# Second FFN product and output projection of three token blocks on 512 columns at a time, in four PSUM banks of their own, in one kernel of a hybrid RWKV-7/S5 layer

## The chip, the cores and the metric

The kernel runs on one core of a Trainium2 chip. The metric is device time in microseconds (us) of one execution. The engines are TensorE (PE in the rows, with PEld for its weight loads), VectorE (DVE), ScalarE (ACT), GpSimd (POOL) and SyncE (SP), whose queue issues the DMAs. PSUM, in which matmuls accumulate, has eight banks, each of 128 partitions x 512 fp32 values.

## The reference, cut to what matters

One layer with the same weights on 256 context tokens and 2048 latent tokens, model width 1024. The mixer has two head groups: a bidirectional RWKV-7 recurrence (8 heads of 64) and a bidirectional S5 with a gated linear unit. Then:

```
# mixer: rwkv_x = (groupnorm(y_fwd + y_bwd) + bonus) * (sigmoid(gd) @ g2); s5_x = z * sigmoid(z @ glu_w + glu_b)
x = x + mod_x[2] * (concatenate([rwkv_x, s5_x], -1) @ w_out)          # w_out 1024 x 1024
h = modulate(rmsnorm(x, norm2_g), mod_x[3], mod_x[4])
x = x + mod_x[5] * ((silu(h @ w1) * (h @ w3)) @ w2)                   # w1, w3 1024 x 2816, w2 2816 x 1024
return rmsnorm(x, final_g)
```

The outputs are the 2048 latent rows in fp32. To keep precision each large product is made of three reduced-precision ones: both factors are split into a high and a low part, and high x high, high x low and low x high are added up in the same bank.

## The kernel before

The change lies in the last part of the program, the class `Tail`. The 2048 latent tokens are taken as four blocks of 512, from block 3 down to block 0. For each block there are these steps:

- **readout(b)**, in eight pieces: reads the scan's result from DRAM (tiles yl, pl, vl), normalises it by heads, adds the bonus and multiplies with the gate. A piece takes three banks: pcv (L1213 on high and low parts for the mean, later transposes), pb and pg.
- **outproj(b)** and **norm(b)**: the product with w_out is added to X1 (the residual, token rows on the partitions), squares are summed on the way, and `rms` makes the reciprocal root. GpSimd puts it on a diagonal (tile nt, L1340), TensorE multiplies it with X1, which also transposes (L1347), VectorE applies scale and shift (L1349) and the result is split into tiles H and L, the ffn's input.
- **ffn(b)**: 22 pieces f of 128 hidden columns. A piece has 2 x 24 matmuls of 512 columns for w1 and w3 (L1371, tiles p), then silu, multiplication and a split into gh and gl. Pieces come in parts, `SPLITS` = f 0-3, 4-7, 8-11, 12-15, 16-19 and 20-21, and each part ends with its share of the second product.
- **final(b)**: the last norm and the store.

Both products, w_out and w2, go through `product`. It walks over the 1024 output columns in four steps of 256 (cq). In a step two banks hold four 128 x 256 results, and each contraction step k loads and splits a 128 x 256 piece of weights (vr, vh, vl2) and issues 4 x 3 matmuls of 256 columns (L1295 to L1297). At the end of a step VectorE multiplies with the gate (L1300) and GpSimd adds into X1 (L1303).

The banks: pool `fp` has four, under one name "f", handed out in the order in which the program asks. The w1/w3 tiles and `product` take theirs there. When the scan's banks have been given up (`rwkv.close()`), `aside` brings four more, pool `fq`; from then on readout and norm of blocks 2 to 0 take theirs from `fq`.

The order of the work: the last twelve units of the RWKV scan (R.unit, L1005 to L1082 among its lines) are written first, then parts 0 to 2 of ffn(3). Then comes, for b = 3, 2, 1: parts 0 to 2 of ffn(b) (unless b is 3), the readout of block b - 1 with parts 3 and 4 of ffn(b) written between its pieces, outproj(b - 1), norm(b - 1), part 5 of ffn(b) and final(b). ffn(0) stands at the end. A scheduler lays out each engine's instruction row from this text before the kernel runs: an instruction may be put ahead of others if its tiles and banks can be had by then, and banks of one pool go to the users in the order of the text. On the chip an engine's row is fixed.

Of the kernel before, what the change touches and what calls it, by code (L numbers as in the profile page):

```python
# [9 lines left out]
F32 = mybir.dt.float32  # L10
F32R = mybir.dt.float32r
I32 = mybir.dt.int32
AF = mybir.ActivationFunctionType
OP = mybir.AluOpType
# [1094 lines left out]
class Tail:  # L1109


    def __init__(self, tc, I, K, S, out, f1, fp):
        self.tc, self.nc, self.I, self.K, self.S, self.out = tc, tc.nc, I, K, S, out
        self.f1, self.fp = f1, fp
        self.side = (f1, fp, "t", "s", "gh", "gl")
        self.C, self.H, self.X = {}, {}, {}
        nc, blk, ident = self.nc, K["blk"], K["ident"]
        self.Cm = f1.tile([P, P], F32, name="Cm")
        nc.vector.scalar_tensor_tensor(self.Cm, blk, -1.0 / 64, ident, op0=OP.mult, op1=OP.add)
        self.RK = f1.tile([P, 4, P], F32, name="RK")  # L1120
        for hp in range(4):
            nc.vector.tensor_scalar(self.RK[:, hp], blk, V(K, "rwkv_rk", hp), None, op0=OP.mult)
        self.gb = f1.tile([P, 4], F32, name="gb")
        o = VOFF["s5_glu_b"]
        nc.vector.tensor_scalar(self.gb, K["vec"][:, o:o + 4], 0.5, None, op0=OP.mult)
        self.g2 = f1.tile([96, 512], F32, name="g2")
        nc.sync.dma_start(self.g2, I["rwkv_g2"][0])

    def aside(self, f2, fq):

        self.side = (f2, fq, "nt", "ns", "zh", "zl")
        nc = self.nc
        self.ER = f2.tile([P, 2, P], F32R, name="ER")
        nc.scalar.activation(self.ER[:, 0], self.Cm, AF.Copy)
        nc.scalar.activation(self.ER[:, 1], self.K["blk"], AF.Copy)
        self.GR = f2.tile([96, 2, 512], F32R, name="GR")
        self.split(self.GR[:, 0], self.GR[:, 1], self.g2)
# [61 lines left out]
    def readout(self, b, put):  # L1199
# [26 lines left out]
        for hf in range(2):  # L1226
# [7 lines left out]
            for hp in range(4):  # L1234
# [35 lines left out]
                put(b, hp, ts, s)  # L1270
                yield

    def product(self, b, A, n, wsrc, grow, last):


        nc, f1 = self.nc, self.f1
        mm = nc.tensor.matmul
        X1 = self.X[b]
        for cq in range(4):
            cols = slice(256 * cq, 256 * cq + 256)  # L1280
            gq = f1.tile([P, 256], F32, name="gq", bufs=2)
            nc.sync.dma_start(gq, bcast_row(grow[cols], 256))
            po = [self.ftile([P, 2, 256]) for _ in range(2)]
            for k in range(n):
                with self.tc.high_priority(offset=1000):
                    raw = f1.tile([P, 256], F32, name="vr", bufs=3)
                    nc.sync.dma_start(raw, wsrc(k, cols))
                    vh = f1.tile([P, 256], F32R, name="vh", bufs=2)
                    vl = f1.tile([P, 256], F32R, name="vl2", bufs=2)
                    self.split(vh, vl, raw)  # L1290
                ah, al = A[k]
                for j in range(4):
                    o = po[j // 2][:, j % 2]
                    js = slice(j * P, (j + 1) * P)
                    mm(o, ah[:, js], vh, start=k == 0 and j % 2 == 0, stop=False)  # L1295
                    mm(o, ah[:, js], vl, start=False, stop=False)  # L1296
                    mm(o, al[:, js], vh, start=False, stop=k == n - 1 and j % 2 == 1)  # L1297
            for u in range(2):
                t = f1.tile([P, 2, 256], F32, name="t", bufs=2)
                nc.vector.tensor_tensor(t, po[u], gq[:, None, :].to_broadcast([P, 2, 256]), op=OP.mult)  # L1300
                for j in range(2):
                    x = X1[2 * u + j][:, cols]
                    nc.gpsimd.tensor_tensor(x, x, t[:, j], op=OP.add)  # L1303
                    if last:
                        self.square(b, 2 * u + j, cq, t[:, j])

    def square(self, b, j, cq, junk):
        if (b, "ss") not in self.X:
            self.X[b, "ss"] = self.f1.tile([P, 4, 4], F32, name="sq", bufs=2)
        x = self.X[b][j][:, 256 * cq:256 * cq + 256]  # L1310
        self.nc.scalar.activation(junk, x, AF.Square, accum_out=self.X[b, "ss"][:, j, cq:cq + 1])  # L1311

    def rms(self, b):
# [19 lines left out]
    def norm(self, b):  # L1333
# [8 lines left out]
        HL = pool.tile([P, 8, 512], F32R, name="L")  # L1342
        self.H[b] = HH, HL
        for kc in range(8):
            pt = self.ftile(None, fq)
            for j in range(4):
                nc.tensor.matmul(pt[:, j * P:(j + 1) * P], self.X[b][j][:, kc * P:(kc + 1) * P], dg[:, j], start=True, stop=True)  # L1347
            tmp = f2.tile([P, 512], F32, name=tag_s, bufs=2)
            nc.vector.tensor_scalar(tmp, pt, mod[:, 4, kc:kc + 1], mod[:, 5, kc:kc + 1], op0=OP.mult, op1=OP.add)  # L1349
            self.split(HH[:, kc], HL[:, kc], tmp)  # L1350
# [59 lines left out]
def hybrid_block(tc, I, out):  # L1410
    with tc.tile_pool(name="dram", bufs=1, space=bass.MemoryType.DRAM) as dp, \
# [50 lines left out]
        with tc.tile_pool(name="f1", bufs=1, side="right") as f1, tc.tile_pool(name="fp", bufs=4, space=PSUM, side="right") as fp:  # L1462
# [13 lines left out]
                R.unit(h, h < 0 or False, pe_add=False)  # L1476
            run(T.ffn(3, SPLITS[:3]))
            rwkv.close()
            with tc.tile_pool(name="f2", bufs=1) as f2, tc.tile_pool(name="fq", bufs=4, space=PSUM) as fq:
                T.aside(f2, fq)  # L1480
                for b in (3, 2, 1):
                    if b < 3:
                        run(T.ffn(b, SPLITS[:3]))
# [33 lines left out]
```

## Time and profile before

| | us |
|---|---|
| median of three runs | 3780.82 |
| lowest, highest | 3780.75, 3784.65 |
| the profiled execution, its own time | 3786.86 |
| span of the profiled execution | 3785.1 |
| TensorE busy in the span | 3332.9 (88%) |
| VectorE busy | 2496.0 (66%) |
| GpSimd busy | 1831.6 (48%) |
| ScalarE busy | 1722.3 (46%) |

The mean granted TensorE clock of the profiled execution is 0.907 of full speed. Times in the rows are counted from the start of the span. A matmul's busy time runs from its start to its modelled end; the next ones may have started by then. In a timeline a row stands for consecutive alike instructions, with the start of the first, the time from there to the end of the last and, after x, their number. The scan ends at about 2317 us; behind it the blocks 2 to 0 fill the rest.

### The profile page before, as it was taken

To read this page: it belongs to the slowest core of one execution; us is meant where nothing else is said; L and a number is where in the kernel's file an instruction comes from. 1 tells how busy PE (TensorE), PEld (TensorE's weight loads), DVE (VectorE), ACT (ScalarE), POOL (GpSimd) and SP (SyncE) were. 2 spreads that over 40 slices of the span, in tenths; PEclk is the share of its full clock that TensorE was granted. 3 is DMA by queue.
4 is the path that set the end of the run, shared out by engine and by line. 5 is a ranking of instruction groups with operands and counts; after the bars stand their busy time and mean duration, and the time that the engine had idled before them with its cause. 6 is when DMAs were issued, how large, how long until landed. Compare 5 with 4: busy or idle time off the path is not lost. (4 is left out here: it accounts for less than half of the span.)

```text
span 3785.1 us, 70325 instructions
## 1 busy us (share of the span) xinstructions
PE 3332.9 (88%) x25311; PEld 2769.1 (73%) x25311; DVE 2496.0 (66%) x4726; ACT 1722.3 (46%) x3787; POOL 1831.6 (48%) x3184
## 2 busy tenths in 40 slices
PE   5798888888677776688899999999999999999998
PEld 3676666666556555566677888888889888988887
DVE  7668777776879978757766656576444854454444
ACT  3575656555344323554555644353333533343333
POOL 3366658576777656467667663323112321221212
PEclk9798989999767787678899999999999999999999
DMA  6654545554334443166533335454333533334333
GB/s 187 186 135 116 147 116 142 134 145 123 91 105 130 134 136 99 48 165 148 136 97 94 104 97 151 121 169 127 99 98 102 176 104 103 105 100 120 103 99 95
DMA packets 789020, 462.34 MB, mean 122 GB/s; under 512 B 182544, under 2 KB 766868, under 8 KB 788672
## 3 DMA queue, kind: packets, MB, share of 16 engines
q1 hardware_dynamic: 788672, 457.85, 43.3%
q8 instruction: 200, 3.28, 0.4%
q14 instruction: 148, 1.21, 0.1%
HBM read 382.34 MB, written 75.36 MB: 121 GB/s over the span
## 5 line engine op out<-in xcount | busy, mean ns | idle before, releaser
L1303 POOL TENSOR_TENSOR X<-X,t 128x256 f32<-128x256 f32 x464 | 379.0, 845 | 970.4 <-DVE t L1300 963.8
L999 POOL TENSOR_TENSOR tmp<-AT,T 128x60 f32<-128x60 f32 (+24 forms) x992 | 398.9, 402 | 186.2 <-DVE AT L992 85.6
L1144 DVE TENSOR_TENSOR wl<-wr,wh 128x512 fp32r<-128x512 f32 x368 | 270.7, 737 | 278.8 <-PE f L1371 238.2
L1001 POOL TENSOR_TENSOR T<-T,tmp 128x60 f32<-128x60 f32 (+24 forms) x992 | 416.7, 420 | 67.4
L1144 DVE TENSOR_TENSOR vl<-vr,vh 128x256 fp32r<-128x256 f32 x480 | 262.3, 550 | 273.9 <-ACT vh L1143 273.4
L1143 ACT ACTIVATE wh<-wr 128x512 fp32r<-128x512 f32 x368 | 232.2, 632 | 408.5 <-PE f L1371 370.3
L1296 PE MATMUL f<-vl,gh 128*128 128x256 f32 x1408 | 396.1, 289 | 13.6 <-DVE vl L1144 13.5
L1371 PE MATMUL f<-H,wh 128*128 128x512 f32 x1408 | 390.1, 396 | 8.3 <-ACT wh L1143 8.0
L1143 ACT ACTIVATE vh<-vr 128x256 fp32r<-128x256 f32 x480 | 199.3, 417 | 430.5 <-PE f L1297 382.3
L1371 PE MATMUL f<-H,wl 128*128 128x512 f32 x1408 | 389.8, 396 | 5.0 <-DVE wl L1144 4.9
L1371 PE MATMUL f<-L,wh 128*128 128x512 f32 x1408 | 390.5, 394 | 0.0
L1297 PE MATMUL f<-vh,gl 128*128 128x256 f32 x1408 | 388.8, 285 | 0.0
L1295 PE MATMUL f<-vh,gh 128*128 128x256 f32 x1408 | 361.6, 287 | 4.3 <-ACT vh L1143 4.2
L255 DVE SCALAR_TENSOR_TENSOR acc<-zb,cw,acc 128x512 f32<-128x512 f32 (+2 forms) x384 | 317.2, 842 | 26.2 <-ACT acc L251 21.3
L1371 PEld LDWEIGHTS f<-H,wl 128*128 128x128 f32 x1408 | 260.1, 188 | 62.8 <-DVE wl L1144 7.1
L1371 PEld LDWEIGHTS f<-L,wh 128*128 128x128 f32 x1408 | 261.7, 188 | 57.3
L1371 PEld LDWEIGHTS f<-H,wh 128*128 128x128 f32 x1408 | 256.9, 188 | 62.3 <-ACT wh L1143 9.5
L1296 PEld LDWEIGHTS f<-vl,gh 128*128 128x128 f32 x1408 | 269.7, 192 | 25.0 <-DVE vl L1144 18.4
L1297 PEld LDWEIGHTS f<-vh,gl 128*128 128x128 f32 x1408 | 269.9, 192 | 2.7
L1295 PEld LDWEIGHTS f<-vh,gh 128*128 128x128 f32 x1408 | 252.7, 191 | 13.1 <-ACT vh L1143 6.3
L222 PE MATMUL pa<-HI,wl 128*128 128x512 f32 (+1 forms) x712 | 208.2, 413 | 59.3 <-POOL wl L219 39.1
L222 PE MATMUL pa<-HI,wh 128*128 128x512 f32 (+1 forms) x712 | 217.6, 428 | 18.4 <-ACT wh L218 12.3
(459 smaller groups left out, 7391.1 us busy)
## 6 DMA issues: line engine op xcount, KB each, us to landing
wr<-in_ffn_w_dram SPq DMA_DIRECT2D x352, 256.0 KB
raw<-in_w_in_dram SPq DMA_DIRECT2D x178, 256.0 KB
vr<-in_ffn_w_dram SPq DMA_DIRECT2D x352, 128.0 KB
ld<-s_rkvk SPq DMA_DIRECT2D x36, 768.0 KB
mraw<-in_mod_w_dram SPq DMA_DIRECT2D x64, 256.0 KB
vr<-in_w_out_dram SPq DMA_DIRECT2D x128, 128.0 KB
gq<-s_gate SPq DMA_DIRECT2D x116, 128.0 KB
SV<-s_vt SPq DMA_DIRECT2D x144, 64.0 KB
```

Of the source, the lines that this page charges most:

```text
L222: nc.tensor.matmul(pa[:, :nt], w[:, kc, :], h[:, 4 * kh + kc, :nt], start=kh + i + kc == 0, stop=kh == 1 and i == 2 and kc == 3)
L255: nc.vector.scalar_tensor_tensor(ag, zb[:, i0 - 1 + a:i0 - 1 + a + nr, e:e + 64], tap(a, e), ag, op0=OP.mult, op1=OP.add)
L999: eng.tensor_tensor(tv, AT[:, l + 1:, l:l + 1].to_broadcast([P, n, m]), T[:, l:l + 1, 0:m].to_broadcast([P, n, m]), op=OP.mult)
L1001: eng.tensor_tensor(T[:, l + 1:, 0:m], T[:, l + 1:, 0:m], tv, op=OP.add)
L1143: self.nc.scalar.activation(hi, x, AF.Copy)
L1144: self.nc.vector.tensor_tensor(lo, x, hi.bitcast(F32), op=OP.subtract)
L1295: mm(o, ah[:, js], vh, start=k == 0 and j % 2 == 0, stop=False)
L1296: mm(o, ah[:, js], vl, start=False, stop=False)
L1297: mm(o, al[:, js], vh, start=False, stop=k == n - 1 and j % 2 == 1)
L1303: nc.gpsimd.tensor_tensor(x, x, t[:, j], op=OP.add)
L1371: mm(p, a[:, kc, :], h[:, 4 * kh + kc, :], start=kh + i + kc == 0, stop=kh == 1 and i == 2 and kc == 3)
```

## The change

`product` gets a second form, `wide`, which all calls for blocks 2 to 0 use once `aside` has run; block 3 keeps the narrow one. `wide` walks over the output columns in two steps of 512. Its four 128 x 512 results each have a bank of their own, o0 to o3, in a pool `fo` that replaces `fq`; each has one buffer. Weights come in 128 x 512 pieces (wr, wh, wl in f2), and a contraction step issues 4 x 3 matmuls of 512 columns. `norm` takes its banks from o0 to o3, too. `readout` of blocks 2 to 0 now takes its banks from `fp`, together with w1 and w3. The sums of squares have two columns for a row of X1 where there were four.

```diff
-    def aside(self, f2, fq):
-
-        self.side = (f2, fq, "nt", "ns", "zh", "zl")
+    def aside(self, f2, fo):
+
+        self.side = (f2, self.fp, "nt", "ns", "zh", "zl")
+        self.fo = fo
...
+    def wide(self, b, A, n, wsrc, grow, last):
+
+        nc, f1, f2 = self.nc, self.f1, self.side[0]
+        mm = nc.tensor.matmul
+        X1 = self.X[b]
+        for cq in range(2):
+            cols = slice(512 * cq, 512 * cq + 512)
+            gq = f2.tile([P, 512], F32, name="gw", bufs=2)
+            nc.sync.dma_start(gq, bcast_row(grow[cols], 512))
+            po = [self.fo.tile([P, 512], F32, name="o%d" % j) for j in range(4)]
+            for k in range(n):
+                with self.tc.high_priority(offset=1000):
+                    raw = f2.tile([P, 512], F32, name="wr", bufs=3)
+                    nc.sync.dma_start(raw, wsrc(k, cols))
+                    vh = f2.tile([P, 512], F32R, name="wh", bufs=2)
+                    vl = f2.tile([P, 512], F32R, name="wl", bufs=2)
+                    self.split(vh, vl, raw)
+                ah, al = A[k]
+                for j in range(4):
+                    js = slice(j * P, (j + 1) * P)
+                    mm(po[j], ah[:, js], vh, start=k == 0, stop=False)
+                    mm(po[j], ah[:, js], vl, start=False, stop=False)
+                    mm(po[j], al[:, js], vh, start=False, stop=k == n - 1)
+            for j in range(4):
+                t = f1.tile([P, 512], F32, name="t", bufs=2)
+                nc.vector.tensor_tensor(t, po[j], gq, op=OP.mult)
+                x = X1[j][:, cols]
+                nc.gpsimd.tensor_tensor(x, x, t, op=OP.add)
+                if last:
+                    self.square(b, j, cq, t, 512)
+
     def product(self, b, A, n, wsrc, grow, last):
 
 
+        if self.fo and b < 3:
+            return self.wide(b, A, n, wsrc, grow, last)
         nc, f1 = self.nc, self.f1
...
-            pt = self.ftile(None, fq)
+            pt = self.fo.tile([P, 512], F32, name="o%d" % (kc % 4)) if self.fo else self.ftile()
...
-            with tc.tile_pool(name="f2", bufs=1) as f2, tc.tile_pool(name="fq", bufs=4, space=PSUM) as fq:
-                T.aside(f2, fq)
+            with tc.tile_pool(name="f2", bufs=1) as f2, tc.tile_pool(name="fo", bufs=1, space=PSUM) as fo:
+                T.aside(f2, fo)
```

The lines of the changed kernel have other numbers: L1213 becomes L1215 (readout), L1371 becomes L1406 (w1 and w3), L1347 becomes L1382 (norm), and L1295 to L1297 are now the wide matmuls.

The change moves instructions on TensorE's row in two places of interest. The first is the end of the scan. Before, w1/w3 matmuls of ffn(3) (L1371, tiles f, H and L with wh and wl) stand between those of the last scan unit (L1014, L1021, L1052):

```order
L1371 MATMUL f<-L,wh 128x512 x4
L1014 MATMUL p<-tmp,AY 32x32 x16
L1371 MATMUL f<-H,wl 128x512 x4
L1371 MATMUL f<-H,wh 128x512 x4
L1371 MATMUL f<-L,wh 128x512 x4
L1371 MATMUL f<-H,wl 128x512 x4
L1371 MATMUL f<-H,wh 128x512 x4
L1371 MATMUL f<-L,wh 128x512 x3
L1021 MATMUL p<-TW_1082,T_22200 32x32 x16
L1371 MATMUL f<-L,wh 128x512
```

After, the same unit's matmuls follow one another directly, and the first of readout(2) (L1215) stand behind them, ahead of the next of ffn(3) (L1406):

```order
L1021 MATMUL p<-TW_1085,T_22529 32x32 x16
L1052 MATMUL p<-R,TW_1085 64x64 x8
L1061 MATMUL c<-UV,BT 64x64 x8
L1074 MATMUL p<-AR,UV 64x64 x8
L1076 MATMUL p<-Q,SV 64x64 x8
L1047 MATMUL c<-SV,Q 64x64 x8
L1052 MATMUL p<-R,TW_1085 64x64 x8
L1074 MATMUL p<-AR,UV 64x64 x8
L1076 MATMUL p<-Q,SV 64x64 x8
L1215 MATMUL f<-rh,ER 128x256 x2
L1215 MATMUL f<-sh,GR 128x256
L1406 MATMUL f<-H,wh 128x512 x4
```

What moved are the w1/w3 matmuls of ffn(3) and the narrow product that belongs to them, from between the scan's matmuls to behind the first readout matmuls.

The second place is the end of outproj(1), TensorE again. Before, w1/w3 and narrow product matmuls of ffn(2) (L1371, and L1295 to L1297 with gh and gl) stand between the last matmul of outproj(1) and the first of norm(1) (L1347):

```order
L1297 MATMUL f_31830<-vh_31959,L_29565 128x256
L1371 MATMUL f_32162<-H_27108,wh_32183 128x512 x2
L1371 MATMUL f_32162<-L_27109,wh_32183 128x512 x4
L1371 MATMUL f_32162<-H_27108,wl_32184 128x512 x4
L1371 MATMUL f_32199<-H_27108,wh_32202 128x512 x4
L1371 MATMUL f_32199<-L_27109,wh_32202 128x512 x4
L1371 MATMUL f_32199<-H_27108,wl_32203 128x512 x4
L1295 MATMUL f_32245<-vh_32249,gh_32158 128x256
```

After, the norm's first matmul (L1382, in bank o0) follows directly on the last wide one of outproj(1) (bank o3):

```order
L1297 MATMUL o2_30429<-wh_30559,L_28789 128x512
L1296 MATMUL o3_30430<-wl_30560,H_28788 128x512
L1297 MATMUL o3_30430<-wh_30559,L_28789 128x512
L1382 MATMUL o0_30613<-nt_30606,X1_30250 128x128
L1382 MATMUL o1_30622<-nt_30606,X1_30250 128x128
```

What moved are the remaining matmuls of ffn(2)'s last part: those of w1 and w3 stand further up, those of its second product behind the norm's.

## Rows read from the trace of the kernel before

**Rows 1.** Stretches, core 0: length, then busy us (count) by engine, clock, DMA.
```profile
core 0: us, PE busy (x) PEld busy (x) DVE busy (x) ACT busy (x) POOL busy (x), PEclk, DMA share, GB/s
2226.00:2324.00 98.00, 97.55 (x885) 82.53 (x885) 47.75 (x88) 42.40 (x94) 50.68 (x124) 1.00 0.33 97
2324.00:2420.00 96.00, 89.33 (x553) 78.37 (x552) 72.46 (x198) 43.52 (x100) 36.64 (x45) 1.00 0.57 168
2420.00:3750.00 1330.00, 1315.47 (x7887) 1164.63 (x7887) 706.84 (x1351) 493.30 (x1080) 313.56 (x390) 1.00 0.39 114
1895.00:1900.00 5.00, 4.47 (x67) 3.99 (x64) 3.19 (x11) 1.66 (x4) 3.02 (x10) 0.55 0.08 22
```

**Rows 2.** Page, costliest groups: busy us, mean ns | idle before, releaser.
```profile
L1296 PE MATMUL f<-vl,gh 128*128 128x256 f32 x1408 | 396.1, 289 | 13.6 <-DVE vl L1144 13.5
...
L1371 PE MATMUL f<-H,wh 128*128 128x512 f32 x1408 | 390.1, 396 | 8.3 <-ACT wh L1143 8.0
```

**Rows 3.** TensorE's timeline, ffn(0): start, us, instruction, count.
```profile
3498.03 1.09 PE L1371 MATMUL f<-L,wh 128*128 128x512 f32 x4
...
3501.76 0.28 PE L1295 MATMUL f<-vh,gh 128*128 128x256 f32 x1
...
3506.21 0.28 PE L1295 MATMUL f<-vh,gh 128*128 128x256 f32 x1
...
3508.13 0.28 PE L1296 MATMUL f<-vl,gh 128*128 128x256 f32 x1
```

**Rows 4.** TensorE's timeline, end of the scan and first readout matmul.
```profile
2253.60 1.18 PE L1014 MATMUL p<-tmp,AY 32*32 32x32 f32 x32
...
2291.79 1.18 PE L1014 MATMUL p<-tmp,AY 32*32 32x32 f32 x32
...
2315.76 0.68 PE L1076 MATMUL p<-Q,SV 64*64 64x64 f32 x16
...
2323.98 0.28 PE L1213 MATMUL f<-rh,ER 128*128 128x256 f32 x1
```

**Rows 5.** Timelines of ScalarE and GpSimd there; in brackets idle time before.
```profile
2250.70 0.69 ACT L1005 ACTIVATE tmp<-T 128x256 f32<-128x256 f32 x1
...
2255.02 0.47 POOL L999 TENSOR_TENSOR tmp<-AT,T 128x31 f32<-128x31 f32 x1 [6.09 <-PE p L1014]
...
2282.05 0.66 ACT L1005 ACTIVATE tmp<-T 128x256 f32<-128x256 f32 x1 [4.46 <-DVE T L1004]
...
2316.48 0.77 ACT L1082 ACTIVATE YW<-p 64x256 f32<-64x256 f32 x2 [0.82 <-PE p L1076]
```

**Rows 6.** TensorE's timeline, a scan unit without filler and norm(3).
```profile
1886.25 0.28 PE L1297 MATMUL f<-vh,L 128*128 128x256 f32 x1
...
1898.64 1.04 PE L1076 MATMUL p<-Q,SV 64*64 64x64 f32 x16
...
1899.62 0.38 PE L1347 MATMUL f<-t,X 128*128 128x128 f32 x1
```

**Rows 7.** TensorE's timeline, end of outproj(1) and start of norm(1).
```profile
2921.64 0.28 PE L1297 MATMUL f<-vh,L 128*128 128x256 f32 x1
...
2921.76 0.63 PE L1371 MATMUL f<-H,wh 128*128 128x512 f32 x2
...
2931.13 0.50 PE L1347 MATMUL f<-nt,X 128*128 128x128 f32 x3
```

**Rows 8.** Timelines of VectorE and GpSimd in the same place.
```profile
2921.36 1.29 DVE L1300 TENSOR_TENSOR t<-f,gq 128x512 f32<-128x512 f32 x2 [0.31 <-PE f L1297]
...
2922.14 3.51 POOL L1303 TENSOR_TENSOR X<-X,t 128x256 f32<-128x256 f32 x4 [22.77 <-DVE t L1300]
...
2933.57 1.53 DVE L1349 TENSOR_SCALAR ns<-f,modv 128x512 f32<-128x512 f32 x2 [0.57 <-PE f L1347]
...
2948.27 0.68 DVE L1144 TENSOR_TENSOR L<-ns,H 128x512 fp32r<-128x512 f32 x1
```

**Rows 9.** TensorE's timeline, its last matmul.
```profile
3768.82 0.28 PE L1297 MATMUL f<-vh,gl 128*128 128x256 f32 x1
```

More of the change, by code (lines that the diff above doesn't have):

```diff
@@ L1115, in __init__ @@
         self.side = (f1, fp, "t", "s", "gh", "gl")
+        self.fo = None
         self.C, self.H, self.X = {}, {}, {}
@@ L1305, in product, with square @@
                         self.square(b, 2 * u + j, cq, t[:, j])
-    def square(self, b, j, cq, junk):
+    def square(self, b, j, cq, junk, n=256):
         if (b, "ss") not in self.X:
-            self.X[b, "ss"] = self.f1.tile([P, 4, 4], F32, name="sq", bufs=2)
-        x = self.X[b][j][:, 256 * cq:256 * cq + 256]
+            self.X[b, "ss"] = self.f1.tile([P, 4, 4], F32, name="sq", bufs=2)[:, :, 0:D // n]
+        x = self.X[b][j][:, n * cq:n * cq + n]
         self.nc.scalar.activation(junk, x, AF.Square, accum_out=self.X[b, "ss"][:, j, cq:cq + 1])
```

## The prediction

> **What bounds the kernel now.** I first read the stretches table [rows 1]. From 2420 us to 3750 us TensorE is busy for 1315.47 of 1330 us at full granted clock, so in the stage that the change rewrites the time is TensorE's pace, and only 14.5 us of idle time are there to win. In 2226 to 2324 us, the end of the scan, it is just as full (97.55 of 98). Behind that, in 2324 to 2420 us, it is idle for 6.7 us. So two questions decide: does the wide product need fewer TensorE us, and does TensorE still find work in the places where it now has none to spare?
>
> The groups table [rows 2] answers the first wrongly if read as it stands: 289 ns for a 256-column matmul and 396 for a 512-column one make 2 x 289 - 396 = 182 ns for each pair replaced, some 390 us over 2160 pairs. These durations overlap, since matmuls are pipelined. The timeline gives the pace from start to start [rows 3]: 16 matmuls of 512 columns take 3501.76 - 3498.03 = 3.73 us, 0.2333 each; 16 of 256 columns take 3508.13 - 3506.21 = 1.92 us, 0.120 each.
>
> **The pace.** Each of blocks 2, 1, 0 has 22 + 8 = 30 contraction steps of 4 x 4 x 3 = 48 narrow matmuls: 4320 in all, which become 2160 wide. A pair costs 0.240 us, a wide one 0.2333: 0.0067 x 2160 = 14.4 us. The small gaps that the narrow stream shows at bank changes add 1 or 2: I take -16, bounds -10 and -22.
>
> Here a page can be set beside the row. The Trainium skill, "TensorE: Matmul & The Clock Gate", section "Back-to-back issue gap", gives 262 cycles for 256 columns and 518 for 512; at 2.4 GHz two minus one is 6 cycles, 2.5 ns, an estimate of 5.4 us for 2160 pairs. The trace shows 6.7 ns where the page has 2.5; the measurement decides, and both are far below the 182 ns of the groups table.
>
> **The end of the scan.** In the trace of before TensorE fills the waits of the last two scan units with the fourth part of ffn(3), f12 to f15 (48 matmuls of 512 each), its narrow product (192 of 256) and 14 matmuls of f16: (192 + 14) x 0.2333 = 48.1, plus 192 x 0.120 = 23.0, together 71.1 us, all ahead of the first readout matmul of block 2 at 2323.98 [rows 4]. After the change the readout takes its banks from the pool of four that ffn uses, and that part of ffn(3) was written behind the first readout step. The first place of the order shows the result: in the new order no ffn matmul stands among the last units' matmuls; L1406 comes only behind L1215. TensorE takes its row in order, so these 71 us are done later, and the scan's end runs bare.
>
> How much earlier does it end, bare? From the rows of the engines beside it [rows 4, 5]: the input of the last but one unit's L1014 is ready at 2250.70 + 0.69 = 2251.4. L1014 and its follower start 1.4 us apart (2253.60 to 2255.02). GpSimd's inverse runs from 2255.02 until ScalarE hands on its result at 2282.05: 27.0, and the copy 0.7. Then L1014 and L1021 of the last unit, in the trace 8.1 us with 28 large matmuls (6.5) between them, bare 2 x 1.18 + 2 x 0.66 = 3.7. Then L1052 to the last L1076: the same chain ran nearly bare before norm(3), from 1886.25 to 1898.64 + 1.04 [rows 6], 13.4. The copy 2316.48 + 0.77, and from there to the first readout matmul, through DRAM, 2323.98 - 2317.25 = 6.7. Sum: 2251.4 + 1.4 + 27.0 + 0.7 + 3.7 + 13.4 + 0.8 + 6.7 = 2305. So the readout starts 19 us earlier and 71.1 us of TensorE work lie behind it: +52. Bounds: +41, if the bare chain ends at 2294 because GpSimd and VectorE, with fewer splits to share, run it a tenth faster; +71, if it ends no earlier.
>
> **The norms.** Between the last outproj matmul of block 1 (2921.64) and the first of its norm (2931.13) lie 9.5 us, in which VectorE scales, GpSimd adds the residual [rows 8], ScalarE squares and the reciprocal root is formed. In the trace TensorE works right through it, on w1/w3 matmuls of ffn(2), in other banks [rows 7]. While VectorE then turns norm banks into the next block's input (2933.57 to 2948.27 [rows 8]), it works on the narrow product of ffn(2).
>
> After the change w1/w3 of f20 and f21 stand ahead of the second half of outproj, and the wide product of ffn(b, last part) needs banks o0 to o3, which the norm takes first. The second place of the order shows the last L1297 with L1382 right behind it; norm(0) has the same. TensorE's only choice is to wait. The price of one: the chain, 9.5, plus 1.5 because four multiplications and four 512-column additions are still to come after the last matmul where two and four narrower ones were, = 11; then some 4 us in the norm phase (eight bank reads at about 0.77 each, with splits between, against 3.74 us of L1347), less the 1.5 that stand there now: 13.5. Twice that is +27. Norm(2) keeps 80 narrow matmuls of block 3 as cover, 9.6 us: +4. The nearest bare row, norm(3), has 13.4 us from its last outproj matmul to its first L1347 [rows 6], so the bounds for all three are +20 and +40.
>
> **Smaller terms.** Readouts now compete with the w1/w3 tiles for four banks, and a readout bank is held through a chain of ScalarE and VectorE steps: +6, bounds 0 and +20 (24 steps of under 1 us). Of the deferred work some can fill the 6.7 us that are idle behind readout(2) [rows 1]: -6, bounds 0 and -10. Where TensorE had been mostly idle the granted clock was 0.55 in the next 5 us (1895 to 1900 [rows 1]), and full in the stage behind: three new idle stretches give +3, bounds 0 and +10. At the end, 16.3 us lie between the last matmul (3768.82 [rows 9]) and the end of the span; four last additions of 512 columns instead of 256 are left over: +1, bounds -1 and +3.
>
> **Costed at nothing.** Weight loads of 256 KB in place of 128, half as many issues on SP: that queue is not late in the stage, and a wide step lasts 24 x 0.2333 = 5.6 us. The splits of a 512 step (about 0.7 us on either engine) run under the same 5.6 us. The o banks are single: at the change of column step four multiplications of 0.69 us stand against the next step's first matmuls, whose bank is the first one freed, 12 matmuls (1.4 to 2.8 us) after it was finished. If that cover failed, it would cost about 1 us at each of some 20 changes; this is in the upper bound.
>
> **The sum**, against the profiled execution's own 3786.86 us: -16 + 52 + 27 + 4 + 6 - 6 + 3 + 1 = +71, 3858. The profiled execution stands 6 us above the median of the runs shown (3780.82), so the forecast is **3852 us**, 1.9% slower.
>
> **Rivals.** (1) *TensorE loses no work time*, the faster side: the deferred 71 us and the norms' waits fit into time that was idle anyway, or TensorE passes by a waiting matmul; only the pace is left, 3781 - 16 = 3765. It decides if idle time behind 2324 us exceeds about 80 us; the rows show 6.7 + 14.5 = 21 [rows 1], and in the bare stretch before norm(3) nothing of another sort ran on TensorE between the chain's matmuls and L1347 [rows 6]. The Trainium skill, "TensorE: Matmul & The Clock Gate", section "Step-by-step: what each phase is for", has matmuls in program order, with only weight loads drawn ahead; the trace agrees there, with 13.4 us between the last outproj matmul and L1347 [rows 6]. Chance 6 in 100.
> (2) *It nets out*: the pace is worth 22, the scan ends 30 us earlier, and the norms are half covered; about 3781, against three rows at once. 3 in 100.
> (3) *Norms covered*: squares, sums and the ident scaling finish under the last matmuls, so that the 31 us fall away; 3820. For it: the multiplications now come in larger pieces. Against it: nothing stands between the two lines in the order. 10 in 100.
> (4) *Worse*: the scan ends no earlier (+71 where I have +52), norms 40, clock 10, readouts 10: 3852 + 19 + 9 + 7 + 4 = 3891, up to some 3900. 14 in 100.
> The forecast itself, 3820 to 3880, has 67.
>
> **How the numbers follow.** About 0.2%, 7.5 us, is what a measurement of this kernel tells from no change. Faster: rival 1, 0.06; same: rival 2, 0.03; slower: the rest, 0.91. For the range, leaving out rivals 1 and 2 and half of rival 4 leaves some 16 in 100 out: 3806 to 3892, of which the lower end stands for the covered norms with a cheaper scan end (3820 less 14).
>
> **What would show it.** In the new trace: the first L1215 of block 2 near 2305 us, with TensorE well under half busy in the 50 us before it; two idle stretches of 10 us or more directly before L1382, and one of about 4; 0.233 us from start to start in the wide stream; TensorE's idle time from there to the end at some 50 to 60 us where it was 21. A first L1215 near 2324 means rival 4, one before 2280 or ffn matmuls among the last scan rows means that the largest term is wrong. No idle time ahead of L1382 means rival 3. A time under 3780 would say that the order on TensorE isn't what sets the time here.

## The result and the profile after

| | before | after |
|---|---|---|
| median, us | 3782.39 (4 runs) | 3829.48 (3826.88 to 3835.88, 4 runs) |
| ratio, 95% interval | | 1.0129, 1.0114 to 1.0145 |
| span of the profiled execution, us | 3785.1 | 3834.0 |
| TensorE busy, us | 3332.9 (88%) | 3312.2 (86%) |

The changed kernel is 47 us slower. The forecast was 71 us slower, 3852, with a range from 3806 to 3892.

The stretches of the changed kernel (columns as in [rows 1]): the first three answer to those of before, the other three lie around the start of norm(1).

```profile
core 0: us, PE busy (x) PEld busy (x) DVE busy (x) ACT busy (x) POOL busy (x), PEclk, DMA share, GB/s
2226.00:2324.00 98.00, 56.74 (x601) 47.58 (x601) 38.98 (x90) 34.74 (x83) 42.52 (x124) 0.76 0.33 105
2324.00:2420.00 96.00, 94.21 (x526) 81.10 (x525) 57.16 (x142) 37.68 (x80) 25.16 (x30) 1.00 0.41 120
2420.00:3750.00 1330.00, 1298.50 (x5897) 1060.20 (x5896) 696.90 (x1201) 452.86 (x837) 286.79 (x244) 0.99 0.38 114
...
2970.00:2975.00 5.00, 0.03 (x1) 0.00 (x0) 2.96 (x3) 2.61 (x7) 3.77 (x4) 0.88 0.30 102
2975.00:2980.00 5.00, 0.70 (x3) 0.70 (x4) 1.96 (x12) 0.91 (x4) 1.78 (x5) 0.50 0.16 44
2980.00:2985.00 5.00, 5.00 (x29) 5.00 (x29) 0.46 (x1) 0.00 (x0) 0.29 (x1) 0.59 0.00 0
```

At the scan's end TensorE works 56.74 of 98 us where it worked 97.55. From 2420 to 3750 us it stands 31.5 us where it stood 14.5.

**The scan's end.** TensorE's timeline of the changed kernel, which answers to [rows 4]; in brackets the idle time before and what ended it:

```profile
2251.36 1.20 PE L1014 MATMUL p<-tmp,AY 32*32 32x32 f32 x32 [13.37 <-ACT tmp L1005]
...
2277.75 1.20 PE L1014 MATMUL p<-tmp,AY 32*32 32x32 f32 x32 [11.11 <-ACT tmp L1005]
...
2281.79 1.12 PE L1052 MATMUL p<-R,TW 64*64 64x64 f32 x16 [0.86 <-ACT TW L1024]
...
2290.57 0.68 PE L1076 MATMUL p<-Q,SV 64*64 64x64 f32 x16
...
2296.41 0.93 PE L1215 MATMUL f<-rh,ER 128*128 128x256 f32 x2 [5.16 <-ACT rh L1145]
```

The three gaps, 13.37, 11.11 and 5.16 us, are what the ffn(3) matmuls filled before. The two executions do not reach this place at the same time, so a common mark is wanted. The same batch of L963 matmuls, ahead of the stretch that the order changes, starts at 2221.99 us in before and at 2224.39 in after:

```profile
2221.99 1.16 PE L963 MATMUL w<-Q,BK 64*128 64x128 f32 x16
```

```profile
2224.39 1.16 PE L963 MATMUL w<-Q,BK 64*128 64x128 f32 x16
```

From this mark the first readout matmul comes after 2323.98 - 2221.99 = 102.0 us in before and 2296.41 - 2224.39 = 72.0 in after: 30.0 earlier, with 71.1 us of work put off. The scan's end costs 41.1 us.

**The norms.** TensorE's timeline at norm(1), which answers to [rows 7]:

```profile
2969.64 0.39 PE L1297 MATMUL o<-wh,L 128*128 128x512 f32 x1
...
2979.30 7.26 PE L1382 MATMUL o<-nt,X 128*128 128x128 f32 x40 [9.27 <-POOL nt L1375]
...
2990.59 1.09 PE L1406 MATMUL f<-L,wh 128*128 128x512 f32 x4
```

The wait of 9.27 us ends with GpSimd's nt; norm(0) has one of 9.31, norm(2) one of 1.18. In the stretch of 5 us in which the wait ends the granted clock is 0.50, in the next 0.59 (stretches above), and 40 norm matmuls take about 7 us where 32 took 3.74 in before. From the end of outproj (2969.9) to 2990.6 lie 20.7 us; in them stand 64 norm matmuls, 7.5 us at the pace of before, and four w1/w3 matmuls, 0.9. So norm(1) loses 12.3 us, norm(0) by the same working 11.8, norm(2) 2.4: together 26.5.

**The product.** The group of the second part of the wide product on the page, which answers to the L1296 row in [rows 2]:

```profile
L1296 PE MATMUL o<-wl,gh 128*128 128x512 f32 x528 | 208.9, 396 | 0.0
```

No idle time stands ahead of it, where before had 13.6 us. Those 13.6 are of the whole execution; 8.5 of them lie behind 2330 us, where the product of blocks 2 to 0 is (the row is shown under the run with five buffers). This was not in my sum, and the experiments come to it last.

The ledger of the two profiled executions (after less before, us):

| | |
|---|---|
| ahead of the mark | +2.4 |
| scan's end (71.1 put off, 30.0 earlier) | +41.1 |
| work behind the first readout matmul, by counts x pace (0.2333, 0.120), without the 71.1 | -14.5 |
| time behind the first readout matmul that is no such work: 87.2 where it was 69.0 | +18.2 |
| last matmul to the end, 17.6 where it was 16.0 | +1.6 |
| sum (span 3834.0 - 3785.1 = 48.9) | +48.8 |

The +18.2 is itself a difference. Take for each matmul the time from the start of the one before it, less the pace of that one, and add up by the matmul that follows: the norms' matmuls give +28.4, those of w1 and w3 +11.5, the wide product +1.4, readouts -1.8, the narrow product -21.3. The pauses alone, places with more than 0.02 us over the pace ahead of a narrow matmul, are 31.2 us behind the first readout matmul in before and 7.0 in after: about 24 us are gone.

### The profile page after: what moved, and what is told of

It is laid out like the page before. It is cut to its first block, busy times and chain, and to the rows that moved or that the text cites. A ratio compares the mean times of both kernels' runs of the same rounds, so it can differ in the third digit from the quotient of the medians.

```text
span 3834.0 us, 64694 instructions
## 1 busy us (share of the span) xinstructions
PE 3312.2 (86%) x23151; PEld 2655.6 (69%) x23151; DVE 2479.2 (65%) x4546; ACT 1676.2 (44%) x3511; POOL 1794.9 (47%) x3016
## 5 line engine op out<-in xcount | busy, mean ns | idle before, releaser
L1146 DVE TENSOR_TENSOR wl<-wr,wh 128x512 fp32r<-128x512 f32 x548 | 438.2, 805 | 424.7 <-ACT wh L1145 223.7
L1302 POOL TENSOR_TENSOR X<-X,t 128x512 f32<-128x512 f32 x168 | 242.2, 1461 | 761.4 <-DVE t L1300 752.5
L1406 PE MATMUL f<-H,wh 128*128 128x512 f32 x1408 | 395.4, 398 | 9.6 <-DVE s L1410 3.3
L1406 PE MATMUL f<-H,wl 128*128 128x512 f32 x1408 | 392.6, 397 | 6.5 <-DVE wl L1146 6.5
L1406 PE MATMUL f<-L,wh 128*128 128x512 f32 x1408 | 391.9, 396 | 0.1
L255 DVE SCALAR_TENSOR_TENSOR acc<-zb,cw,acc 128x512 f32<-128x512 f32 (+2 forms) x384 | 317.4, 843 | 28.3 <-ACT acc L251 23.5
L1406 PEld LDWEIGHTS f<-H,wh 128*128 128x128 f32 x1408 | 262.2, 189 | 71.4 <-ACT rh L1223 3.8
L1406 PEld LDWEIGHTS f<-H,wl 128*128 128x128 f32 x1408 | 263.8, 189 | 68.7 <-DVE wl L1146 9.1
L1406 PEld LDWEIGHTS f<-L,wh 128*128 128x128 f32 x1408 | 265.2, 189 | 61.0 <-DVE L L1146 0.5
L222 PE MATMUL pa<-LO,wh 128*128 128x512 f32 (+1 forms) x712 | 206.5, 410 | 3.3 <-DVE LO L202 3.3
L1296 PE MATMUL o<-wl,gh 128*128 128x512 f32 x528 | 208.9, 396 | 0.0
L1297 PE MATMUL o<-wh,gl 128*128 128x512 f32 x528 | 201.2, 395 | 0.0
L222 PEld LDWEIGHTS pa<-HI,wl 128*128 128x128 f32 x712 | 136.7, 211 | 92.9 <-POOL wl L219 43.7
L1295 PE MATMUL o<-wh,gh 128*128 128x512 f32 x528 | 198.0, 397 | 0.6 <-ACT gh L1145 0.3
L970 ACT ACTIVATE AX<-w 32x128 f32<-32x128 f32 x288 | 115.5, 401 | 171.2 <-DVE Q L967 167.8
L1300 DVE TENSOR_TENSOR t<-o,gw 128x512 f32<-128x512 f32 x168 | 113.3, 686 | 103.3 <-PE o L1297 72.0
L222 PEld LDWEIGHTS pa<-HI,wh 128*128 128x128 f32 x712 | 140.1, 216 | 51.2 <-ACT wh L218 16.3
```

What stands on the lines that cost most here:

```text
L222: nc.tensor.matmul(pa[:, :nt], w[:, kc, :], h[:, 4 * kh + kc, :nt], start=kh + i + kc == 0, stop=kh == 1 and i == 2 and kc == 3)
L255: nc.vector.scalar_tensor_tensor(ag, zb[:, i0 - 1 + a:i0 - 1 + a + nr, e:e + 64], tap(a, e), ag, op0=OP.mult, op1=OP.add)
L970: act(AX[i % 2][r0:r0 + 32, :, b0:b0 + 4].rearrange("p i b -> p b i"), ps[par][r0:r0 + 32, :, c0:c0 + 32], AF.Copy, scale=-0.5)
L1146: self.nc.vector.tensor_tensor(lo, x, hi.bitcast(F32), op=OP.subtract)
L1295: mm(po[j], ah[:, js], vh, start=k == 0, stop=False)
L1296: mm(po[j], ah[:, js], vl, start=False, stop=False)
```

## Experiments

Each kernel was timed beside the kernel before anew, whose median differs by up to 9 us between these sets; so a gain or a loss is read from the ratio, which is taken within one set.

### Readouts in the pool of w1 and w3, nothing else

```diff
-        bank = lambda: self.ftile([P, 256], self.side[1])
+        bank = lambda: self.ftile([P, 256])
...
-                pcv = self.ftile([P, 2, 256], self.side[1])
+                pcv = self.ftile([P, 2, 256])
```

> The kernel before with one thing changed: readouts of blocks 2 to 0 take their banks from the pool of w1/w3 and the product stays narrow. Theory (the order at the end of the scan costs, whatever the product's width): the scan's end runs bare as in the changed kernel, the first readout matmul of block 2 near 2295 us with 71 us of ffn(3) behind it, so about 41 us slower than before, 3823 us (3815 to 3832, of which up to 8 are for the two later readouts' competition for banks). Rival (the wide product itself is what is slow): within 5 us of the kernel before, 3782.

Measured: 3848.51 us against 3788.30 for the kernel before on the same chip, ratio 1.0163 (1.0147 to 1.0178), 61 us slower. A kernel with no wide product in it is as slow as the changed one, and slower. So the readouts' banks cost by themselves, and the rival (the wide product is what is slow) is out. The size missed: 61 where I expected 33 to 50.

### The same for readout(2) alone

```diff
-        bank = lambda: self.ftile([P, 256], self.side[1])
+        bank = lambda: self.ftile([P, 256], None if b == 2 else self.side[1])
...
-                pcv = self.ftile([P, 2, 256], self.side[1])
+                pcv = self.ftile([P, 2, 256], None if b == 2 else self.side[1])
```

> The kernel before with the banks of readout(2) alone taken from the w1/w3 pool; readouts of blocks 1 and 0 keep their own four. Theory: the bare end of the scan alone, 41 us slower than before (36 to 48); the run with all three readouts in that pool was 61 us slower, so the two later readouts cost the other 15 to 20 in the narrow kernel, where readout, w1/w3 and the product share four banks. Rival (the end of the scan costs it all): within 5 us of that run, some 60 slower.

Measured: 3831.99 us against 3791.11, ratio 1.0103 (1.0087 to 1.0120): 39 us by the ratio, 41 by the medians. The bare end of the scan costs 41 by the ledger. Its first readout matmul stands 72.0 us behind its mark, as in the changed kernel, and time behind it that is no work is 69.0 us, the same as in before:

```profile
2293.13 0.93 PE L1213 MATMUL f<-rh,ER 128*128 128x256 f32 x2 [5.16 <-ACT rh L1143]
```

The two later readouts cost the other 20 us or so in the run above, in a kernel where readout, w1/w3 and the narrow product share four banks. In the changed kernel the product isn't among them.

### The changed kernel with readout(2) in the o banks

```diff
+    def ob(self):
+        self.oi = getattr(self, "oi", -1) + 1
+        return self.oi % 4
...
-        bank = lambda: self.ftile([P, 256], self.side[1])
+        bank = lambda: (self.fo.tile([P, 512], F32, name="o%d" % self.ob())[:, 0:256] if self.fo and b == 2 else self.ftile([P, 256], self.side[1]))
...
-                pcv = self.ftile([P, 2, 256], self.side[1])
+                pcv = (self.fo.tile([P, 512], F32, name="o%d" % self.ob()).rearrange("p (a c) -> p a c", a=2) if self.fo and b == 2 else self.ftile([P, 2, 256], self.side[1]))
```

> The changed kernel with the banks of readout(2) alone taken from o0 to o3, where nothing else is wanted at that time. Theory: ffn(3)'s f12 to f15 stand among the last scan units again, so the 41 us come back: 3829 - 41 = 3788 us (3780 to 3796), and the two idle stretches of 9.3 us ahead of norm(1) and norm(0) stay. Rival (the wide product is what is slow): 3829 within 5.

Measured: 3791.85 us against 3788.30, ratio 1.0005 (0.9995 to 1.0015). All of the scan's cost comes back (47 us between the two ratios), and the wait at norm(1) is still there, to the hundredth:

```profile
2318.72 0.28 PE L1219 MATMUL o<-rh,ER 128*128 128x256 f32 x1
...
2933.81 7.29 PE L1386 MATMUL o<-nt,X 128*128 128x128 f32 x40 [9.27 <-POOL nt L1379]
```

In this kernel the new waits, most of them at the norms, and the product's gain are about equal.

### The last part of ffn(2) and ffn(1) narrow again

```diff
-        if self.fo and b < 3:
+        if self.fo and b < 3 and not (b and n == 2):
             return self.wide(b, A, n, wsrc, grow, last)
```

> The changed kernel with the narrow product, in the w1/w3 pool, for the last part (f20, f21) of ffn(2) and ffn(1) alone. Theory: these matmuls stand between outproj and norm again and cover the chain: two idle stretches of 9.3 us go, and with them the low clock behind them (about 2.5 us each), less 0.7 us for 96 pairs of narrow matmuls: 3829 - 22 = 3807 us (3803 to 3813). Rival (another engine is as late, so that the idle time only moves): 3829 to 3822.

Measured: 3836.15 us against 3788.30, ratio 1.0129 (1.0114 to 1.0145), the same as the changed kernel. The edit did what it should to the order, but gained nothing: the rival was right. Four timelines of this kernel at norm(1), TensorE's, VectorE's, GpSimd's and ScalarE's:

```profile
2977.18 0.39 PE L1297 MATMUL o<-wh,L 128*128 128x512 f32 x1
2983.60 0.55 PE L1330 MATMUL f<-vh,gh 128*128 128x256 f32 x1 [6.02 <-DVE t L1335]
...
2995.22 5.11 PE L1382 MATMUL o<-nt,X 128*128 128x128 f32 x40
```

```profile
2982.76 0.69 DVE L1335 TENSOR_TENSOR t<-f,gq 128x512 f32<-128x512 f32 x1 [1.53 <-ACT t L1346]
```

```profile
2980.71 2.48 POOL L1302 TENSOR_TENSOR X<-X,t 128x512 f32<-128x512 f32 x2 [1.23 <-DVE t L1300]
```

```profile
2982.01 0.63 ACT L1346 ACTIVATE t<-X 128x512 f32<-128x512 f32 x1 [1.77 <-POOL X L1302]
```

The narrow product needs a tile t for its multiplication (L1335). The two t tiles are held by outproj until GpSimd has added (L1302) and ScalarE has squared into them (L1346). So the cover waits for the chain that it was to cover, 6.02 us, and its additions then queue on GpSimd ahead of the norm's own step: the first norm matmul comes 17.8 us behind the last of outproj (2995.22 against 2977.4), where it came 9.3 behind. That t is the cause is read from these releasers; a kernel with more t tiles was not run.

### Both edits together

The diffs are the two above.

> Both edits together, readout(2) in the o banks and the last part of ffn(2) and ffn(1) narrow. Theory: the two costs are separate and add up: 3829 - 41 - 22 = 3766 us (3760 to 3775), that is 0.2 to 0.6% faster than the kernel before, the pace of the wide matmuls being what is left. Rival (the wide product costs by its single banks and longer weight loads what its pace gains): 3780 to 3790.

Measured: 3801.29 us against 3788.30, ratio 1.0037 (1.0024 to 1.0049), 9 us worse than the readout edit alone. The expectation failed with that of the run before: it took 22 us for the narrow last part, which is worth nothing or less. Its rival's time, up to 3790, was passed as well.

### Outproj narrow again, with readout(2) in the o banks

```diff
-        if self.fo and b < 3:
+        if self.fo and b < 3 and n != 8:
             return self.wide(b, A, n, wsrc, grow, last)
```

> The changed kernel with readout(2) in the o banks (as in the run with that edit alone) and outproj narrow as before, in the w1/w3 pool; all of ffn(2) to ffn(0) is wide. 66 of 90 contraction steps are wide. With outproj holding two w1/w3 banks at a time, matmuls of f20 and f21 are left over ahead of the norms, 7.9 us by the order. Theory: of the norms' some 24 us 18 come back, and 24 x 24 pairs lose 4: 14 us faster than with the readout edit alone, 10 faster than before, a ratio of 0.996 to 0.9985. Rival (as with the last part made narrow: the wait moves behind another engine): 1.000 to 1.003.

Measured: 3771.10 us against 3791.11, ratio 0.9941 (0.9928 to 0.9953): 22 us faster than the kernel before by the ratio, 24 better than with the readout edit alone by the two ratios, where I expected 14. TensorE's timeline at norm(1):

```profile
2918.04 0.28 PE L1336 MATMUL f<-vh,L 128*128 128x256 f32 x1
...
2925.16 1.10 PE L1410 MATMUL f<-H,wl 128*128 128x512 f32 x4
2926.10 3.77 PE L1386 MATMUL o<-nt,X 128*128 128x128 f32 x32
```

Narrow outproj holds w1/w3 banks, so w1/w3 matmuls are left over for the 7.9 us behind its last matmul, and the norm starts with no wait and at full pace (32 in 3.77 us). W1/w3 matmuls use no t tile and nothing of GpSimd: this cover works where the last one didn't. Between the profiled executions of the readout edit and of this kernel, added up from start to start as in the ledger, the time ahead of norm matmuls fell by 25.4 us and that ahead of w1/w3 matmuls by 9.5, which I had not counted, and the work grew by 4. The norms' term is confirmed at some 25 us of the changed kernel's time.

### The wide product only where it needs nobody's bank

`wide` in the kernel before, with its banks from the second pool of four, which readout and norm keep; used for ffn(0) and for parts 0 to 2 of ffn(2) and ffn(1):

```diff
-            po = [self.fo.tile([P, 512], F32, name="o%d" % j) for j in range(4)]
+            po = [self.ftile(None, self.side[1]) for j in range(4)]
...
+    def product(self, b, A, n, wsrc, grow, last, far=False):
...
+        if far:
+            return self.wide(b, A, n, wsrc, grow, last)
...
+            self.product(b, G, f1_ - f0, lambda k, cols: self.I["ffn_w2"][0, (f0 + k) * P:(f0 + k + 1) * P, cols], self.S["gate"][1], f1_ == NF, b == 0 or b < 3 and f0 < 12)
```

> The kernel before with the wide product only where it needs no other user's bank: all of ffn(0) and parts 0 to 2 of ffn(2) and ffn(1), in the second pool of four, which readout and norm keep; outproj and parts 3 to 5 of ffn(2) and ffn(1) stay narrow. 46 of 90 contraction steps are wide, 1104 pairs. The order leaves f12 to f15 among the last scan units and 9.4 us of other matmuls ahead of each norm. Theory: only the pace is left, 1104 x 6.7 to 8 ns = 7 to 9 us faster than before, a ratio of 0.9976 to 0.9981. Rival (the wide product's larger weight loads, splits or banks take the gain back): 0.999 to 1.002.

Measured: 3782.62 us against 3791.11, ratio 0.9976 (0.9966 to 0.9985), 9 us faster, as the pace has it. Time behind the first readout matmul that is no work stayed at 69.2 us: the pauses ahead of narrow matmuls were 28.3 us here and 31.2 in before, though the narrow stream behind that matmul is about half as long. So half of the wide product alone, with no bank moved, is a small gain, and it took few of the pauses away.

### Five buffers for the split weights of the narrow product

```diff
+        pl, nb = (f1, 2) if self.side[0] is f1 or b == 3 else (self.side[0], 5)
...
-                    vh = f1.tile([P, 256], F32R, name="vh", bufs=2)
-                    vl = f1.tile([P, 256], F32R, name="vl2", bufs=2)
+                    vh = pl.tile([P, 256], F32R, name="vh", bufs=nb)
+                    vl = pl.tile([P, 256], F32R, name="vl2", bufs=nb)
```

> The kernel before with five buffers instead of two for the split weights vh and vl2 of the narrow product of blocks 2 to 0; the product stays narrow and all banks stay where they were. It asks for the size of a gain that the forecast left out: before, TensorE stands 14.6 us, in 31 stops, ahead of narrow matmuls behind the first readout matmul, waiting mostly for VectorE's split, and in the changed kernel 5 us. Theory (the wide step's longer cover, 5.6 us against 2.9, removed these stops): with five buffers ready ahead they go here too, some 8 of the 14.6 us lying in blocks 2 to 0, so 5 to 9 us faster than before, a ratio of 0.9976 to 0.9987. Rival (VectorE itself is late there, however many buffers there are): 0.999 to 1.001, with the stops still in the trace.

Measured: 3761.88 us against 3785.05, ratio 0.9931 (0.9913 to 0.9949): 23 to 26 us faster, some three times what I expected, with not one matmul made wide. Its median is the lowest here, but the interval of its ratio overlaps with that of the kernel with outproj narrow (0.9928 to 0.9953). Three things differ from before: the number of buffers, the pool of the tiles, and TensorE's order, which the scheduler made anew for five buffers: in ffn(0) 186 narrow matmuls follow one another from 3486.40 us on, where before has 150 in a row and 36 more in pieces between w1/w3 matmuls. The groups of TensorE from 2330 to 3830 us, of before and of this kernel (busy us, mean ns | idle before; the lines of this kernel have numbers one higher):

```profile
L1296 PE MATMUL f<-vl,gh 128*128 128x256 f32 x1152 | 320.5, 287 | 8.5 <-DVE vl L1144 8.4
```

```profile
L1297 PE MATMUL f<-vl,gh 128*128 128x256 f32 x1152 | 321.6, 281 | 3.2 <-DVE vl L1144 3.2
```

By the idle column 5 us went. From start to start more went, because a pause shorter than the modelled tail of a matmul leaves no idle time. A step of the kernel before, on TensorE's timeline:

```profile
2843.72 0.28 PE L1297 MATMUL f<-vh,gl 128*128 128x256 f32 x1
2844.15 0.50 PE L1295 MATMUL f<-vh,gh 128*128 128x256 f32 x2
2844.61 0.39 PE L1296 MATMUL f<-vl,gh 128*128 128x256 f32 x1
2844.83 0.28 PE L1297 MATMUL f<-vh,gl 128*128 128x256 f32 x1
```

Start to start these are 0.43, 0.46 for two, and 0.22, where 0.12 each is usual: 0.6 us lost, and no bracket shows any of it. Behind 2500 us before has 20.0 us of pauses ahead of narrow matmuls, in 110 places, and this kernel has 4.8, in 22 (counted as in the ledger). Time behind the first readout matmul that is no work by the paces of before fell from 69.0 to 42.4.

The steady pace is another, too. Twelve matmuls of a step in before take 2848.78 - 2847.34 = 1.44 us, in this kernel 2843.41 - 2842.01 = 1.40, 0.1167 each, half of 0.2333:

```profile
2847.34 0.40 PE L1295 MATMUL f<-vh,gh 128*128 128x256 f32 x2
...
2848.78 0.40 PE L1295 MATMUL f<-vh,gh 128*128 128x256 f32 x2
```

```profile
2842.01 0.28 PE L1296 MATMUL f<-vh,gh 128*128 128x256 f32 x1
...
2843.41 0.28 PE L1296 MATMUL f<-vh,gh 128*128 128x256 f32 x1
```

At this pace two narrow matmuls cost what a wide one does. But it isn't the pool alone that sets it. In the same execution outproj(1) has this pace, 2861.49 - 2860.09 = 1.40 us for twelve, and outproj(0) has the old one, 3301.64 - 3300.20 = 1.44, with vh and vl2 in f2 both times:

```profile
2860.09 0.28 PE L1298 MATMUL f<-vh,L 128*128 128x256 f32 x1
...
2861.49 0.28 PE L1298 MATMUL f<-vh,L 128*128 128x256 f32 x1
```

```profile
3300.20 0.28 PE L1298 MATMUL f<-vh,L 128*128 128x256 f32 x1
...
3301.64 0.28 PE L1298 MATMUL f<-vh,L 128*128 128x256 f32 x1
```

In before it is the other way round: on average 0.120 in outproj(1) and 0.118 in outproj(2) and outproj(0), leaving out the pauses. The stationary tiles H and L are another block's each time, so the places of both factors may matter; no run changes those of H and L.

### Two buffers, in the other place

The diff is the one above with 2 in place of 5.

> As the run with five buffers for vh and vl2, with two buffers as before: only the place of these tiles is another (pool f2 in place of f1), and the order on TensorE is the one before. With five buffers 23 us went, of which some 15 by a narrow pace of 0.117 us from start to start instead of 0.120 behind the first readout, some 10 by shorter pauses at the steps. Theory A (place decides the pace, number of buffers the pauses): pace 0.117, a ratio of 0.995 to 0.9975, the pauses stay. Theory B (ready buffers decide both): pace 0.120, 0.999 to 1.001.

Measured: 3789.26 us against 3787.28, ratio 1.0002 (0.9993 to 1.0011). Half of each theory held. The pace is 0.117 behind 2500 us, outproj(0) excepted (0.120), as theory A has it: a step from 3521.40 to 3522.80 takes 1.40 us.

```profile
3521.40 0.39 PE L1296 MATMUL f<-vh,gh 128*128 128x256 f32 x2
...
3522.80 0.39 PE L1296 MATMUL f<-vh,gh 128*128 128x256 f32 x2
```

But the time is that of theory B. The pauses behind 2500 us grew from 20.0 us (110 places) to 25.5 (147): what the faster pace gave, the waits for the next weights took. As far as these sums tell, with two buffers the narrow stream goes by the arrival of split weights, not by TensorE. So the gain of the run above needs the five buffers, with the order that they bring; what share that order has, no run tells.

## Why the prediction was right, and what missed in it

**Direction and cause.** The two large costs that the forecast named are there at the places it named, and each went with its own edit: the scan's end with readout(2)'s banks (41 us by the ledger; 39 where it was added to the kernel before, 47 by the two ratios where it was taken from the changed one), the norms with narrow outproj (24 between two runs). The rival that TensorE passes by a waiting matmul, or finds room for 71 us of put-off work, was wrong; TensorE stood still in the gaps of 13.37 and 11.11 us, with 71 us of ffn(3) further down its row. Nor were the norms covered. Of the rival in which it nets out two rows of three came true (the scan's end 30 us earlier, the product worth more than 22), and only the third, half covered norms, did not.

**Scan's end: +52, measured +41.1**, my lower bound. The error is in the durations of the bare chain. Counted from the mark, its first L1014 started 2.4 us earlier than I had. I had 29.1 us from one L1014 to the next (1.4 + 27.0 + 0.7); it took 2277.75 - 2251.36 = 26.4. There the condition of my lower bound held, that GpSimd runs faster with fewer splits beside it: from GpSimd's first step to ScalarE's result are 2277.06 - 2253.60 = 23.5 us where before had 27.0, with VectorE idle for 10.48 of them:

```profile
2253.60 0.25 POOL L999 TENSOR_TENSOR tmp<-AT,T 128x31 f32<-128x31 f32 x1 [3.65 <-DVE TW L1008]
```

```profile
2277.06 0.64 ACT L1005 ACTIVATE tmp<-T 128x256 f32<-128x256 f32 x1 [9.94 <-DVE T L1004]
```

```profile
2276.39 0.64 DVE L1004 STREAM_TRANSPOSE T<-T 128x256 f32<-128x256 f32 x1 [10.48 <-POOL T L1001]
```

That the missing splits are the reason is not shown by a run. From the last L1014 to the first readout matmul I had 3.7 + 13.4 + 0.8 + 6.7 = 24.6; it took 18.7, of which L1052 to the end of the last L1076 are 9.5 where I took 13.4 from the stretch before norm(3), [rows 6], and from there to the readout 5.2 where I had 7.5. The row of norm(3) covers work that ran beside outproj(3) and a chain with more in it; as an analogue it was too slow. The clock did fall (0.76 in the mean of the stretch), and still the chain was faster than with ffn(3) matmuls between its steps.

**Norms: +31, measured 26.5.** A wait of 9.27 and 9.31 where I had 11, some 3 us more for a low clock and the norm's own waits where I had 2.5; norm(2) 2.4 where I had 4.

**Pace: -16, measured -14.5 and another -24.** This is the step that failed. The argument was that a 256-column matmul takes 0.120 us from start to start and half of a 512-column one 0.1167, so that width is worth 0.0067 us a pair. The run with five buffers has narrow matmuls at 0.1167: the difference is not one of width alone. And I counted the pauses of the narrow product by small gaps worth 1 or 2 us, while [rows 2] had 13.5 us of idle time ahead of L1296 with VectorE's vl as releaser (8.4 of it behind 2330 us), and more was hidden under modelled ends: 14.6 us idle ahead of all narrow matmuls from 2330 us on, 31.2 from start to start. Two buffers of 512 columns reach 2 x 2.8 us ahead, two of 256 only 2 x 1.44. What the width itself is worth stays open: with two buffers each, the wide form in half of the steps gained 9 us where the narrow form in the same pool, in all of them, gained none, and five narrow buffers gained 23 to 26. (The forecast, and the expectation of the run with five buffers after it, gave a wide contraction step 24 matmuls and 5.6 us; it has 12 and 2.8 us. The splits, 0.7 us, fit into that as well, and nothing hung on it.) The busy share of 1315.47 in 1330 us, from which I took that only 14.5 us were to be won, was no bound: the run with five buffers won 23 to 26.

**Small terms: +3, and the remainder of the ledger is +16.** (48.9 - 2.4 - 41.1 - 26.5 + 14.5 + 24.2 - 1.6.) The new waits stand ahead of w1/w3 matmuls: 11.5 us, of which 6.3 fall in the first 30 us behind the first readout matmul, where matmuls ran slow (four w1/w3 ones in 1.9 us). Ahead of readout matmuls there is no more waiting than before (1.8 us less), so the +6 for their competition is not seen there. The rest is the wide product's 1.4 and the two ways of counting, at the norms (26.5 or 28.4) and in the narrow product (24.2 or 21.3). The end was +1.6 for +1.

Together the scan's end was 11 too dear, the norms 4 and the product's gain 23 too small, against 13 on the small terms; with the 2.4 ahead of the mark, 71 became 49 between the profiled executions and 47 by the medians. The two large waits were foreseen with their places; that the total came within 22 us is in part luck, since the 13 us of waits that no term held made up for a third of what the three other terms were off the other way. The signs tell the same: the first L1215 came at 2296 us, not near 2305, the idle stretches ahead of L1382 were 9.27, 9.31 and 1.18 us, not 10 or more twice and about 4, and TensorE's idle time from 2324 us on was 33 us where I had 50 to 60. What cannot be told apart by these runs: why the place of vh and vl2 changes the pace by 3% in most parts and the other way in outproj(2) and outproj(0), and how the new waits ahead of w1/w3 matmuls divide between banks and the clock.

## What to carry to other kernels

Moving a tile to another bank pool changes what the scheduler may put into a wait: look in the order for what used to fill the waits of a serial chain, before counting what the change saves. Cover for a chain should not need the chain's own tiles and engines: narrow product matmuls did not help, by the releasers since their multiplication and addition waited for the chain's tiles and stood in the same queues, and w1/w3 matmuls did. Before making an instruction larger, try more buffers for its operand; here that gave 0.7%, with another pool for these tiles and the order that the scheduler then made.

## What the runs showed of the hardware

- A busy TensorE by the profile can hide pauses: a matmul of 256 columns is drawn 0.28 us long and the next one can start 0.12 us behind it, so a pause of up to 0.16 us shows as no idle time, and one of 0.43 us from start to start (2843.72 to 2844.15 in before), which leaves 0.15, showed no bracket either. Start-to-start times show them.
- The pace of the same 256-column matmuls was 0.120 us with the moving tile in one pool of SBUF and 0.117 in another, with two buffers each and the same pattern of order; the pool is the only difference made. Outproj(2) and outproj(0) went the other way, from 0.118 to 0.120, so the moving tile's pool alone does not set it.
- With 9.27 us of no matmul (2970.03 to 2979.30 in the changed kernel) the granted clock read 0.88, 0.50 and 0.59 in the stretches of 5 us from 2970, 2975 and 2980 us, and the 64 norm matmuls, with short waits and four w1/w3 matmuls among them, took 11.3 us; with cover ahead of them the first 32 took 3.77.
- Kernels whose edits lie behind it reach the same mark up to 14 us apart (2216.8 to 2230.5), so profiles are to be compared from a mark, not from zero.
